# Where weight pieces begin, modulo 512 bytes, in a two-layer decoder trunk

## The chip, the core and the metric

The kernel runs on one core of a Trainium2 chip. The metric is the device time of one execution in microseconds (us). The kernel before was timed three times on one chip; the median is 609.84 us (609.62 to 609.87).

## The reference

Two identical layers and one final RMSNorm, on 256 tokens of 1024 channels in float32. Each layer reads one normalised input through one wide projection, runs three attention branches on it, and merges them with gates. Cut to what matters:

```python
def hybrid_layer(x, gain, w_in, f_bias, w_branch, w_out):
    h = rms_norm(x, gain)
    proj = jnp.einsum('bsd,de->bse', h, w_in)              # [256,1024] x [1024,9808]
    (qa, ka, va, ga, qb, kb_, vb_, gb, qc, kc, vc, gc,
     q_idx, k_idx, w_idx, f_logit, merge_logit) = jnp.split(proj, SPLIT_POINTS, axis=-1)
    oa = moba_attention(rope(qa), rope(ka), va) * silu(ga)
    ob = dsa_attention(rope(qb), rope(kb_), vb_, rope(q_idx), rope(k_idx), w_idx) * silu(gb)
    oc = forgetting_attention(qc, kc, vc, log_sigmoid(f_logit + f_bias)) * silu(gc)
    y = jnp.einsum('nbsw,nwd->bsnd', jnp.stack([oa, ob, oc]), w_branch)   # 3 x [512,1024]
    merged = jnp.sum(sigmoid(merge_logit).reshape(B, S, 3, D) * y, axis=2)
    return x + jnp.einsum('bsd,de->bse', merged, w_out)    # [1024,1024]
```

Each branch has 8 heads of 64 channels.

## The kernel before, in words

**Numbers in two pieces.** Every operand of a large matmul is split in a "hi" piece (rounded to TensorE's float32r) and a "lo" piece (what is left). A product is three matmuls: hi times hi, lo of the activations times hi of the weights, and hi of the activations times lo of the weights. The activations lie in `hTh` and `hTl` (normalised input), `og0h` to `og1l` (gated branch outputs) and, for the output projection, in the space of `V` (`v0`, `v1`). A weight piece is made from a loaded chunk `raw`: ScalarE writes the hi piece into a buffer `wh` (line 415), VectorE writes the lo piece into a buffer `wl` (line 419). There are six buffers of each, used in turn.

**Which operand stands still.** In `PE.matmul(out, a, b)` the array first loads `a`, 128 columns (the stationary operand; the profile shows this load as a row of its own, LDWEIGHTS on PEld), and then streams `b` past it (the moving operand). A row of the profile names the moving operand first: `proj<-hTh,wh` streams `hTh` past a weight piece, `proj<-wh,v` streams a weight piece past activations.

The kinds of units, by the letters that the change uses:

- B (`unit_b` on `win_b`; queries, keys, gates, indexer and merge logits): a weight piece is stationary, 256 columns of `hTh` or `hTl` move. Per layer 1,536 matmuls. `UNIT_ORDER` mixes hi and lo: six matmuls on hi pieces, one on lo, three on hi, one on lo, and so on.
- Y (`unit_y` on `wbr`; the branch projections): a weight piece is stationary, 256 columns of `og` move. Per layer 288.
- V (values of two branches) and O (output projection; O0 its left half of columns, O1 its right half), both `unit_a` on `rows_a`: activations are stationary, 512 columns of a weight piece move. At the very end, in the right half of the last layer, the second half of the tokens is done in two times 256 columns.
- C and CK (`va_units`; values of the third branch, 256 columns, and its other half with the small projections, 336 columns): activations are stationary, a weight piece moves (line 1132).

Between these stand the matmuls of attention: scores (lines 678 and 680), transposes of the probabilities in threes (line 766), and probabilities times values (lines 782 to 785).

**Where things begin.** The pool lays the buffers one behind the other in each partition. `wh0` begins at byte 1152, which is 128 modulo 512, and each buffer has 1152 words = 4608 = 9 x 512 bytes, so all `wh` begin at 128 and all `wl`, which come 384 bytes later than a multiple of that, at 0. By the same sum `V` and the queries begin at 128, and `hTh`, `hTl`, `og`, the block-diagonal keys `bd` and the transposed probabilities at 192 modulo 512. A buffer has 128 words more than a piece of 1024 words needs, so a piece can be moved inside it. `shifted` does that for moving pieces by the table `MOVING`; stationary pieces take the default, the buffer's start: hi at 128, lo at 0.

**What sets the order.** A planner (`Plan.run`) places every operation on an engine by costs, keys and a table `SHIFT`. It knows no addresses, so places inside a buffer do not enter it.

Of the kernel before, what the change touches and what calls it, by code (L numbers as in the profile page):

```python
# [32 lines left out]

R_RING = 6
R_RAW = 4
MOVING = {"V": (192, 192), "C": (128, 0), "CK": (384, 384), "O": (128, 128)}
TAIL = {"ACT": 95.0, "DVE": 85.0, "POOL": 0.0, "PE": 0.0, "SP": 0.0}
STEP = 24.0
SPLIT_LEAD = 2.0
# [237 lines left out]
def hybrid_trunk(ctx, tc, x, w_in, w_branch, w_out, final_gain, consts, out):  # L277
    nc = tc.nc
    PE, ACT, DVE, POOL = nc.tensor, nc.scalar, nc.vector, nc.gpsimd
# [13 lines left out]
    def T(b):  # L293
        return b.slot[1]
# [28 lines left out]
    V = [pool.tile([128, 2, 8, 128], F32R, name=f"v{i}") for i in range(2)]  # L323
# [67 lines left out]

    chunks, pieces = {}, {}

    def shifted(kind):
        at = MOVING[kind]
        return [slice((a - base) % 512 // 4, (a - base) % 512 // 4 + 1024) for a, base in zip(at, (128, 0))]

    def piece(key, ckey, ap, cshape, sel, shape, k, at=(slice(0, 1024), slice(0, 1024))):
        if key in pieces:
            return pieces[key]  # L400
        if ckey not in chunks:
            c = chunks[ckey] = Buf("raw")
            ca, cb = cshape

            def load():
                c.v = T(c)[:, :ca * cb].rearrange("p (a b) -> p a b", a=ca)
                nc.sync.dma_start(c.v, ap)
            dma(load, 512 * ca * cb * (1 if cb >= 128 else 2), [], [c], k - 12, f"dma {ckey}")
        c = chunks[ckey]
        a, b = shape  # L410
        p = pieces[key] = (Buf("wh"), Buf("wl"))

        def hi():
            p[0].v = T(p[0])[:, at[0]][:, :a * b].rearrange("p (a b) -> p a b", a=a)
            ACT.activation(p[0].v, sel(c.v), AF.Copy)  # L415

        def lo():
            p[1].v = T(p[1])[:, at[1]][:, :a * b].rearrange("p (a b) -> p a b", a=a)
            DVE.tensor_tensor(p[1].v, sel(c.v), p[0].v.bitcast(F32), op=ALU.subtract)  # L419
        act(hi, a * b, False, [c], [p[0]], k - SPLIT_LEAD, f"hi {key}")  # L420
        dve(lo, a * b, [c, p[0]], [p[1]], k - SPLIT_LEAD, f"lo {key}", port=True)
        return p
# [6 lines left out]
    def rows_a(kind, w, l, c0, i, k):  # L429
        src = w[l][(i // 2) * 512:(i // 2 + 1) * 512, c0:c0 + 512].rearrange("(k p) c -> p k c", p=128)  # L430
        a = (i % 2) * 2
        return piece((kind, l, c0, i), (kind, l, c0, i // 2), src, [4, 512], lambda r: r[:, a:a + 2, :], [2, 512], k,
                     shifted("O" if kind == "O" else "V"))

    def wbr(l, n, j, k):
        src = w_branch[l][n][:, (j // 2) * 256:(j // 2 + 1) * 256].rearrange("(k p) c -> p k c", p=128)
# [26 lines left out]
    def unit(name):  # L463
        units[0] += 1
        return units[0] - 1
# [560 lines left out]
    hA = (lambda k, t: hTh[:, k, t * 128:(t + 1) * 128], lambda k, t: hTl[:, k, t * 128:(t + 1) * 128])  # L1026
# [16 lines left out]

    def first_v():

        us, at = [unit("va0"), unit("va1")], shifted("V")
        ps = [Buf("proj"), Buf("proj")]
        left, done = [24, 24], [[], []]
        raws = [Buf("raw"), Buf("raw")]
        for i in range(KC):  # L1050
            c = raws[i // 4]
            if i % 2 == 0:
                ph, pl = Buf("wh"), Buf("wl")
            v = lambda b, w, i=i: T(b)[:, at[w]][:, (i % 2) * 512:(i % 2 + 1) * 512]
            rv = lambda c=c, i=i: T(c)[:, (i % 4) * 512:(i % 4 + 1) * 512]
            src = w_in[0][i * 128:(i + 1) * 128, COL["va"]:COL["va"] + 512]
            kr, kh, kl = Tok(), Tok(), Tok()
            plan.op([("SP", 512 * 512 / 330.0, lambda rv=rv, src=src: nc.sync.dma_start(rv(), src))], [], [kr], -95 + 0.2 * i, LAND,
                    f"dma va{i}", touch=[c])
            key = W_KEY[0] + W_KEY[1] * i  # L1060
            if i:
                key = max(key, HT_KEY[0] + HT_KEY[1] * (i - 0.5))
            plan.op([("ACT", t_act(512, False), lambda v=v, rv=rv, ph=ph: ACT.activation(v(ph, 0), rv(), AF.Copy)),
                     ("DVE", t_dve2(512), lambda v=v, rv=rv, ph=ph: DVE.tensor_copy(v(ph, 0), rv()))],
                    [kr], [kh], key, 0.0, f"hi va{i}", touch=[c, ph])
            dve(lambda v=v, rv=rv, ph=ph, pl=pl: DVE.tensor_tensor(v(pl, 1), rv(), v(ph, 0).bitcast(F32), op=ALU.subtract),
                512, [kr, kh], [kl], key + 0.05, f"lo va{i}", touch=[c, ph, pl], port=True)
            for t in range(2):
                for w, h, kw, kx, n in ((ph, hA[0], kh, 0, 0), (ph, hA[1], kh, 1, 0), (pl, hA[0], kl, 0, 1)):
                    def emit(t=t, w=w, h=h, i=i, v=v, n=n):  # L1070
                        left[t] -= 1
                        PE.matmul(T(ps[t]), h(i, t), v(w, n), start=left[t] == 23, stop=left[t] == 0)  # L1072
                    k = Tok()
                    done[t].append(k)
                    pe(emit, t_mm(512), [kw, k_hT[kx][t][i]], [k], us[t] - 10, f"va{t}", touch=[ps[t], w])
        for t in range(2):
            v_out(ps[t], t, 0, done[t], us[t])

    def va_units(l, vi):

        fine = False
        us, ats = [unit(f"vc{h}{t}") for h in "lr" for t in range(2)], [shifted("C"), shifted("CK")]

        def rows(raw, c, n, k0, k1, key):
            tok = Tok()
# [4 lines left out]
            return tok  # L1090

        def split(p, n, w, c, x0, x1, raw, cols, k0, reads, toks, key):
            dst = lambda i: T(p[i])[:, ats[w > 256][i]][:, :n * w].rearrange("p (k c) -> p k c", k=n)[:, x0:x1, c:c + cols]
            src = lambda: T(raw)[:, :8 * cols].rearrange("p (k c) -> p k c", k=8)[:, k0 + x0:k0 + x1]
            m = (x1 - x0) * cols
            ways = [("ACT", t_act(m, False), lambda: ACT.activation(dst(0), src(), AF.Copy))]
            if fine:
                ways.append(("DVE", t_dve2(m), lambda: DVE.tensor_copy(dst(0), src())))
            plan.op(ways, reads + [k_hT[1][0][KC - 1]], toks[0], key, 0.0, "hi va", touch=[raw, p[0]])
            dve(lambda: DVE.tensor_tensor(dst(1), src(), dst(0).bitcast(F32), op=ALU.subtract), m, reads + toks[0], toks[1],  # L1100
                key + 0.5, "lo va", touch=[raw, *p], port=True)

        for side, (w, slots) in enumerate(((256, ((0, 4), (4, 8))), (336, ((0, 3), (3, 6), (6, 8))))):
            u = us[2 * side:2 * side + 2]
            ps = [Buf("proj"), Buf("proj")]
            left, done = [24, 24], [[], []]
# [9 lines left out]
            for i, (a, b) in enumerate(slots):  # L1116
                p, n = [Buf("wh"), Buf("wl")], b - a
                tk = [[Tok() for _ in range(n)] for _ in range(2)]
                hk = VA_HI[2 * side + i] if fine else u[0] - SPLIT_LEAD
                for x0, x1 in ((0, 2), (2, 4)) if fine and not side and not i else ((0, n),):  # L1120
                    split(p, n, w, 0, x0, x1, raw, 256, a, list({id(kr[a + x]): kr[a + x] for x in range(x0, x1)}.values()),
                          [tk[0][x0:x1], tk[1][x0:x1]], hk)
                kt2 = [[Tok()], [Tok()]]
                if side:
                    split(p, n, w, 256, 0, n, rk, 80, a, [kk], kt2, hk)
                for t in range(2):
                    for wi, hi in ((0, 0), (0, 1), (1, 0)):
                        for js in [(x,) for x in range(n)] if fine and not side and not i else (range(n),):
                            def emit(t=t, wi=wi, hi=hi, js=js, p=p, n=n, a=a, w=w, ps=ps, left=left):
                                for x in js:  # L1130
                                    left[t] -= 1
                                    PE.matmul(T(ps[t])[:, :w], hA[hi](a + x, t), T(p[wi])[:, ats[w > 256][wi]][:, :n * w].rearrange(  # L1132
                                        "p (k c) -> p k c", k=n)[:, x], start=left[t] == 23, stop=left[t] == 0)
                            k = Tok()
                            done[t].append(k)
                            pe(emit, len(js) * (t_mm(w) + 4.6), [tk[wi][x] for x in js] + (kt2[wi] if side else []) +
                               [k_hT[hi][t][a + x] for x in js], [k], u[t] - (10 if fine else 0), f"v{side}{t}", touch=[ps[t], p[wi]])
# [44 lines left out]
    for l in range(L):  # L1182
# [31 lines left out]
        for hh in range(2):  # L1214
            gets = [lambda k, i=i: rows_a("O", w_out, l, hh * 512, i, k) for i in range(4)]
            for t in range(2):
                ra = [lambda k, p=p: [k_mg[k][p]] for p in range(2)]
                cols = [(0, 256), (256, 256)] if last and hh + t == 2 else [(0, 512)]
                for i, (c, n) in enumerate(cols):
                    u, ps = unit_a(f"o{hh}{t}", gets, t, mA[0], mA[1], ra, c, n)  # L1220
# [38 lines left out]
```

## Time and profile before

| what | value |
|---|---|
| median of 3 runs | 609.84 us |
| the profiled execution's own time | 609.88 us |
| its span, first to last instruction | 607.9 us |
| mean granted TensorE clock | 0.998 |
| TensorE matmuls | 4848 records, busy 599.9 us |
| VectorE, ScalarE, GpSimd busy | 534.3, 439.9, 89.7 us |
| DMA moved | 107.39 MB, 177 GB/s in the mean |

The end of a matmul is modelled in this profile: a row's duration runs past the start of the next matmul, and reads about 163 ns more than the step from one start to the next. So rates are read here from starts: the step from one matmul's start to the next one's. In the timeline a row with "x4" is four like matmuls in one line, and the step is the next row's start less its own, over four.

### The profile page before, as it was taken

Reading aid. Unit: us, or ns where it says so; the run is one execution under the profiler, and the core shown is the slowest. Engines: PE = TensorE matmul, PEld = TensorE weight load, DVE = VectorE, ACT = ScalarE, POOL = GpSimd, SP = SyncE. Lnnn points to the kernel's source line nnn. Section 1 sums busy time; section 2 is a strip of 40 time slices with the busy share of each in tenths; the row PEclk is TensorE's granted clock in tenths of the full one; section 3 lists DMA queues with packets and bytes.
Section 4 is the critical chain, followed back from the end, with each engine's and each line's share of the span. In section 5 each row is a group of like instructions: output and inputs, shape, how many; then the busy total and the mean of one; then the engine's idle time right before and its main releaser. Section 6 shows DMA issues by size and latency. Waiting matters only on the chain.

```text
span 607.9 us, 12752 instructions
## 1 busy us (share of the span) xinstructions
PE 599.9 (99%) x4848; PEld 581.7 (96%) x4848; DVE 534.3 (88%) x1340; ACT 439.9 (72%) x933; POOL 89.7 (15%) x97
## 2 busy tenths in 40 slices
PE   8999999999999999999999999999999999999996
PEld 6999999999998999999889999999999999999985
DVE  8899999997998899979586999999889978999873
ACT  6668669697986678775585875987788756986641
POOL 1032052000000334100000520320000014220000
PEclk9999999999999999999999999999999999999999
DMA  9995384845454655284547547557448256445411
GB/s 305 296 312 183 90 240 140 252 134 188 140 174 139 208 173 173 88 274 163 160 141 255 159 139 234 166 183 228 128 118 278 92 175 204 144 139 183 165 35 70
DMA packets 98109, 107.39 MB, mean 177 GB/s; under 512 B 4352, under 2 KB 88960, under 8 KB 98048
## 3 DMA queue, kind: packets, MB, share of 16 engines
q1 hardware_dynamic: 97760, 106.15, 55.4%
q8 instruction: 38, 0.62, 0.4%
q10 hardware_dynamic: 288, 0.43, 0.2%
q14 instruction: 23, 0.19, 0.1%
HBM read 103.42 MB, written 1.05 MB: 172 GB/s over the span
## 4 chain that ended last, share of the span: by engine, by line
PE 97%; issue 1%; DMA 1%; DVE 0%; ACT 0%; POOL 0%; POOLq 0%; DVEq 0%; SPq 0%
PE proj L457 80%; PE proj L1132 4%; PE t L766 3%; PE s L680 2%; PE s L678 2%; PE proj L1072 2%; PE o L785 1%; PE o L782 1%; DMA xg<-in_x_dram 1%; PE o L784 0%; PE o L783 0%; PE t L580 0%; PE s L580 0%; POOL fsum L626 0%; ACT tmp L565 0%
## 5 line engine op out<-in xcount | busy, mean ns | idle before, releaser
L457 PE MATMUL proj<-hTh,wh 128*128 128x256 f32 x1024 | 266.6, 278 | 0.0
L457 PE MATMUL proj<-hTl,wh 128*128 128x256 f32 x1024 | 265.8, 277 | 0.0
L419 DVE TENSOR_TENSOR wl<-raw,wh 128x1024 fp32r<-128x1024 f32 x180 | 221.9, 1240 | 29.1 <-ACT wh L415 26.5
L457 PE MATMUL proj<-hTh,wl 128*128 128x256 f32 x1024 | 230.6, 278 | 0.0
L415 ACT ACTIVATE wh<-raw 128x1024 fp32r<-128x1024 f32 x180 | 190.0, 1058 | 54.9 <-PE proj L457 50.2
L457 PEld LDWEIGHTS proj<-hTh,wh 128*128 128x128 f32 x1024 | 192.4, 188 | 0.1
L457 PEld LDWEIGHTS proj<-hTl,wh 128*128 128x128 f32 x1024 | 192.3, 188 | 0.1
L457 PEld LDWEIGHTS proj<-hTh,wl 128*128 128x128 f32 x1024 | 173.5, 188 | 0.0
L507 POOL TENSOR_TENSOR rsh<-rsh,cst 128x256 f32<-128x256 f32 x40 | 32.9, 823 | 323.4 <-DVE rsh L506 271.5
L509 POOL TENSOR_TENSOR rr<-rr,rsh 128x256 f32<-128x256 f32 x40 | 48.0, 1199 | 5.1 <-DVE rr L508 2.0
L743 ACT ACTIVATE e<-e,st 128x128 f32<-128x128 f32 (+1 forms) x96 | 42.7, 447 | 6.6 <-DVE st L739 6.3
L457 PE MATMUL proj<-wh,v 128*128 128x512 f32 (+1 forms) x144 | 35.2, 366 | 0.0
L457 PE MATMUL proj<-og0l,wh 128*128 128x256 f32 x128 | 33.8, 276 | 0.0
L457 PE MATMUL proj<-og0h,wh 128*128 128x256 f32 x128 | 32.3, 276 | 0.0
L457 PEld LDWEIGHTS proj<-wh,v 128*128 128x128 f32 x144 | 25.3, 189 | 4.2
L457 PE MATMUL proj<-og0h,wl 128*128 128x256 f32 x128 | 28.6, 276 | 0.0
L771 DVE TENSOR_TENSOR ptl<-t,pth 128x384 fp32r<-128x384 f32 x48 | 24.8, 550 | 0.7 <-ACT pth L769 0.5
L457 PEld LDWEIGHTS proj<-og0h,wh 128*128 128x128 f32 x128 | 24.0, 188 | 0.0
L457 PEld LDWEIGHTS proj<-og0l,wh 128*128 128x128 f32 x128 | 24.0, 188 | 0.0
L800 DVE TENSOR_TENSOR ot<-o,ot 64x256 f32<-64x256 f32 x48 | 19.9, 415 | 3.8 <-ACT ot L798 3.4
L769 ACT ACTIVATE pth<-t 128x384 fp32r<-128x384 f32 x48 | 21.8, 482 | 0.4
L457 PEld LDWEIGHTS proj<-og0h,wl 128*128 128x128 f32 x128 | 21.7, 188 | 0.0
(225 smaller groups left out, 1098.5 us busy)
## 6 DMA issues: line engine op xcount, KB each, us to landing
raw<-in_w_in_dram SPq DMA_DIRECT2D x74, 1024.0 KB, 5.3
raw<-in_w_branch_dram SPq DMA_DIRECT2D x24, 512.0 KB, 3.6
raw<-in_w_out_dram SPq DMA_DIRECT2D x8, 1024.0 KB, 5.1
raw<-in_w_in_dram SPq DMA_DIRECT2D x8, 256.0 KB, 5.4
tmp<-wf SPq DMA_DIRECT2D x16, 128.0 KB, 6.5
raw<-in_w_in_dram SPq DMA_DIRECT2D x2, 320.0 KB, 7.6
x<-in_x_dram SPq DMA_DIRECT2D x2, 256.0 KB, 4.9
acc<-in_final_gain_dram SPq DMA_DIRECT2D x1, 512.0 KB, 3.6
```

The lines of the kernel that those rows point to most:

```text
L415: ACT.activation(p[0].v, sel(c.v), AF.Copy)
L419: DVE.tensor_tensor(p[1].v, sel(c.v), p[0].v.bitcast(F32), op=ALU.subtract)
L457: PE.matmul(o(), a(), b(), start=first and i == 0, stop=last and i == n - 1)
L507: gps(lambda: POOL.tensor_tensor(T(sh)[:np_], T(sh)[:np_], s[:np_], op=ALU.mult), S, [k_rope], [sh], key, "rope")
L509: gps(lambda: POOL.tensor_tensor(T(r)[:np_], T(r)[:np_], T(sh)[:np_], op=ALU.add), S, [sh], [r], key, "rope")
L678: PE.matmul(o.rearrange("p (h c) -> p h c", h=2), qh[:, sl], kl[:, :, :n], start=True, stop=False)
L743: act(lambda t=t, a=a, n=n, e=e, st=st: ACT.activation(T(e)[:, a:a + n], T(e)[:, a:a + n], AF.Exp, bias=T(st)[:, t:t + 1], scale=-1.0, acc ...
L766: PE.transpose(T(ps)[:, i * 128:(i + 1) * 128], T(es[h])[:, i * 128:(i + 1) * 128], ident)
L769: act(lambda h=h, src=src: ACT.activation(T(ph)[:, h], src(), AF.Copy), 384, True, [ps], [kp[h][0]], key, "pT", touch=[ph])
L771: dve(lambda h=h, src=src: DVE.tensor_tensor(T(pl)[:, h], src(), T(ph)[:, h].bitcast(F32), op=ALU.subtract), 384, [ps, kp[h][0]], [kp[h][1 ...
L800: dve(lambda r=r, h=h: DVE.tensor_tensor(T(t)[r], T(o)[:64, h * S:(h + 1) * S], T(t)[r], op=ALU.add), S, [o], [kt[h]], key, "og", touch=[t ...
L1132: PE.matmul(T(ps[t])[:, :w], hA[hi](a + x, t), T(p[wi])[:, ats[w > 256][wi]][:, :n * w].rearrange("p (k c) -> p k c", k=n)[:, x], start=le ...
```

## The change

The table `MOVING` becomes `PLACE`, with an entry for every kind of unit and, in each, one pair (hi, lo) for layer 0 and one for layer 1. `piece` looks its own place up by kind and layer; `place` stands for `shifted`, and O is told apart by its half.

What begins elsewhere, in bytes modulo 512 (hi, lo):

| kind | before, both layers | layer 0 now | layer 1 now |
|---|---|---|---|
| B and Y (stationary) | 128, 0 | 128, 128 | 0, 0 |
| C (moving, 256 columns) | 128, 0 | 0, 0 | 128, 128 |
| O1 (moving) | 128, 128 | 128, 128 | 192, 192 |
| V, CK, O0 (moving) | 192, 192; 384, 384; 128, 128 | the same | the same |

Of the 4,832 matmuls 1,944 have an operand that begins elsewhere. Every engine has the same instructions in the same order with the same waits; no size, no count and no buffer changes. The transfers and what they load are the same too, since `raw` is untouched.

```diff
-MOVING = {"V": (192, 192), "C": (128, 0), "CK": (384, 384), "O": (128, 128)}
+PLACE = {"V": ((192, 192), (192, 192)),
+         "C": ((0, 0), (128, 128)),
+         "CK": ((384, 384), (384, 384)),
+         "O0": ((128, 128), (128, 128)),
+         "O1": ((128, 128), (192, 192)),
+         "B": ((128, 128), (0, 0)),
+         "Y": ((128, 128), (0, 0))}
...
-    def shifted(kind):
-        at = MOVING[kind]
-        return [slice((a - base) % 512 // 4, (a - base) % 512 // 4 + 1024) for a, base in zip(at, (128, 0))]
-
-    def piece(key, ckey, ap, cshape, sel, shape, k, at=(slice(0, 1024), slice(0, 1024))):
+    def place(kind, l):
+        at = PLACE[kind][l]
+        return [slice((a - base) % 512 // 4, 1152) for a, base in zip(at, (128, 0))]
+
+    def piece(key, ckey, ap, cshape, sel, shape, k):
+        at = place(key[0] if key[0] in PLACE else "V", key[1])
...
-        return piece((kind, l, c0, i), (kind, l, c0, i // 2), src, [4, 512], lambda r: r[:, a:a + 2, :], [2, 512], k,
-                     shifted("O" if kind == "O" else "V"))
+        return piece((f"{kind}{c0 // 512}" if kind == "O" else kind, l, c0, i), (kind, l, c0, i // 2), src, [4, 512], lambda r: r[:, a:a + 2, :], [2, 512], k)
...
+        def rows_of(p, i, n, w):
+            at = place("C" if w == 256 else "CK", l)[i]
+            return T(p[i])[:, at][:, :n * w].rearrange("p (k c) -> p k c", k=n)
...
-            dst = lambda i: T(p[i])[:, ats[w > 256][i]][:, :n * w].rearrange("p (k c) -> p k c", k=n)[:, x0:x1, c:c + cols]
+            dst = lambda i: rows_of(p, i, n, w)[:, x0:x1, c:c + cols]
```

More of the change, by code (lines that the diff above doesn't have):

```diff
@@ L1044, in first_v @@
     def first_v():
-        us, at = [unit("va0"), unit("va1")], shifted("V")
+        us, at = [unit("va0"), unit("va1")], place("V", 0)
         ps = [Buf("proj"), Buf("proj")]
@@ L1081, in va_units @@
         fine = False
-        us, ats = [unit(f"vc{h}{t}") for h in "lr" for t in range(2)], [shifted("C"), shifted("CK")]
+        us = [unit(f"vc{h}{t}") for h in "lr" for t in range(2)]
+        def rows_of(p, i, n, w):
+            at = place("C" if w == 256 else "CK", l)[i]
+            return T(p[i])[:, at][:, :n * w].rearrange("p (k c) -> p k c", k=n)
         def rows(raw, c, n, k0, k1, key):
@@ L1131, in emit @@
                                     left[t] -= 1
-                                    PE.matmul(T(ps[t])[:, :w], hA[hi](a + x, t), T(p[wi])[:, ats[w > 256][wi]][:, :n * w].rearrange(
-                                        "p (k c) -> p k c", k=n)[:, x], start=left[t] == 23, stop=left[t] == 0)
+                                    PE.matmul(T(ps[t])[:, :w], hA[hi](a + x, t), rows_of(p, wi, n, w)[:, x], start=left[t] == 23, stop=left[t] == 0)
                             k = Tok()
```

## The prediction

> **What bounds the kernel now.** I read the page first, then the chain of waits, then matmul starts in the timeline.
>
> ```profile
> span 607.9 us, 12752 instructions
> PE 599.9 (99%) x4848; PEld 581.7 (96%) x4848; DVE 534.3 (88%) x1340; ACT 439.9 (72%) x933; POOL 89.7 (15%) x97
> PEclk9999999999999999999999999999999999999999
> PE 97%; issue 1%; DMA 1%; DVE 0%; ACT 0%; POOL 0%; POOLq 0%; DVEq 0%; SPq 0%
> ```
>
> TensorE is the chain from end to end, at full clock, and stands waiting for nobody after the start. So the time is the number of matmuls times the step from one to the next, and a place that alters this step alters the time by just that. Nearly all matmuls that the change touches are these, in the view by groups of one shape (name, shape, count, busy us, mean ns):
>
> ```profile
> L457 PE MATMUL proj<-hTh,wh 128*128 128x256 f32 x1024 | 266.6, 278 | 0.0
> L457 PE MATMUL proj<-hTl,wh 128*128 128x256 f32 x1024 | 265.8, 277 | 0.0
> L457 PE MATMUL proj<-hTh,wl 128*128 128x256 f32 x1024 | 230.6, 278 | 0.0
> L457 PE MATMUL proj<-og0l,wh 128*128 128x256 f32 x128 | 33.8, 276 | 0.0
> L766 PE MATMUL t<-cst,e 128*128 128x128 f32 x144 | 21.6, 272 | 0.0
> L785 PE MATMUL o<-ptl,v 128*64 128x256 f32 x48 | 13.5, 281 | 0.0
> ```
>
> They go at one of two steps. The short step is in this long piece of the chain (start, length, count):
>
> ```profile
> 104.45 15.65 PE proj L457 x138
> ```
>
> 15.65 / 138 = 113.4 ns; hi at 128 and lo at 0 alternate, and the moving operand is at 192. The long step is seen behind the transposes of an attention head (timeline; start, duration):
>
> ```profile
> 160.06 0.36 PE L457 MATMUL proj<-hTh,wh 128*128 128x256 f32 x1
> 160.26 0.28 PE L457 MATMUL proj<-hTl,wh 128*128 128x256 f32 x1
> 160.38 0.28 PE L457 MATMUL proj<-hTh,wh 128*128 128x256 f32 x1
> 160.49 0.28 PE L457 MATMUL proj<-hTl,wh 128*128 128x256 f32 x1
> 160.61 0.28 PE L457 MATMUL proj<-hTh,wh 128*128 128x256 f32 x1
> 160.73 0.28 PE L457 MATMUL proj<-hTl,wh 128*128 128x256 f32 x1
> 160.85 0.28 PE L457 MATMUL proj<-hTh,wl 128*128 128x256 f32 x1
> ...
> 161.32 0.28 PE L457 MATMUL proj<-hTh,wl 128*128 128x256 f32 x1
> 161.43 0.28 PE L457 MATMUL proj<-hTl,wh 128*128 128x256 f32 x1
> ```
>
> From 160.26 to 160.85 are five steps in 0.59 us, 117.5 to 118 ns each, and they do not get faster. From 161.32 on, after lo pieces, it is 0.11 again. Behind a score the long step ends with the first lo pieces:
>
> ```profile
> 50.61 0.45 PE L678 MATMUL s<-bd0l,qh 128*128 128x512 f32 x1
> 50.90 0.28 PE L680 MATMUL s<-bd0h,qx 128*128 128x256 f32 x1
> ...
> 51.14 0.28 PE L457 MATMUL proj<-hTh,wh 128*128 128x256 f32 x1
> 51.26 0.28 PE L457 MATMUL proj<-hTl,wh 128*128 128x256 f32 x1
> 51.38 0.39 PE L457 MATMUL proj<-hTh,wl 128*128 128x256 f32 x2
> 51.60 0.28 PE L457 MATMUL proj<-hTh,wh 128*128 128x256 f32 x1
> ```
>
> 51.14 to 51.38 is 0.12 a step; the two on `wl` take 0.22 together. So I read the trace as two rhythms, both of which can hold: a stationary load and the moving stream beside it either fit or hinder each other. The load of the next weights runs beside the stream:
>
> ```profile
> 116.88 0.28 PE L457 MATMUL proj<-hTl,wh 128*128 128x256 f32 x1
> 116.99 0.28 PE L457 MATMUL proj<-hTh,wh 128*128 128x256 f32 x1
> 116.99 0.19 PEld L457 LDWEIGHTS proj<-hTl,wh 128*128 128x128 f32 x1
> ```
>
> An event (a score, a transpose, probabilities times values, a stretch of another shape) throws TensorE into the hindered rhythm. **In every stretch that I looked through, stationary pieces at 128 alone never led out of it once it had settled; pieces at 0 did, mostly within one or two.**
>
> That the relation of the two places matters is also in rows of other units of 256 columns, which never reach the short step:
>
> ```profile
> 21.24 0.63 PE L1132 MATMUL proj<-wh,hTh 128*128 128x256 f32 x4
> 21.71 0.64 PE L1132 MATMUL proj<-wh,hTl 128*128 128x256 f32 x4
> 22.18 0.64 PE L1132 MATMUL proj<-wl,hTh 128*128 128x256 f32 x4
> 22.65 0.63 PE L1132 MATMUL proj<-wh,hTh 128*128 128x256 f32 x4
> 597.02 0.64 PE L457 MATMUL proj<-wh,v 128*128 128x256 f32 x4
> 597.50 0.40 PE L457 MATMUL proj<-wl,v 128*128 128x256 f32 x2
> ...
> 601.34 0.64 PE L457 MATMUL proj<-wh,v 128*128 128x256 f32 x4
> ```
>
> C (moving at 128 or 0, stationary at 192): 0.47 / 4 = 117.5 ns. The end of O1 (both at 128): 0.48 / 4 = 120 ns, and still so 36 matmuls later (601.34 - 597.02 = 4.32 us).
>
> **The change part by part.**
>
> *Work of ScalarE and VectorE.* They write the same pieces elsewhere; nothing is added. Were they a little slower, TensorE's cover is that it does not wait for them now; I cost it at nothing.
>
> *B and Y in layer 0: lo goes from 0 to 128.* Every stationary piece then stands at 128, and the way out of the hindered rhythm is gone. A layer has 3,072 / 2 = 1,536 B and 288 Y matmuls, 1,824 in all. A long step costs 117.5 - 113.3 = 4.2 ns. How many are there? A layer has 16 scores (12 pairs of heads, 4 indexer units), 12 products with values (48 / 4) and 24 triples of transposes (144 / 6); some 43 stretches of B or Y lie between them. Stretches behind a score, a product with values, C/CK or V (1,164 of layer 0's 1,824 matmuls) all begin in the hindered rhythm. Of those behind transposes (the other 660) some four in ten go straight to the short step when they begin on pieces at 128 (both counts are from the starts in the timeline). So 1,164 + 0.6 x 660 = 1,560 long steps, 6.5 us. What is long already must be taken off: the mean duration of B is 277.7 ns against 276 of the `og` row, 1.7 x 3,072 = 5.2 us, of which about 40 steps of 0.20 instead of 0.11 behind transposes (160.06 to 160.26) are some 3.2 us and stay; 2.0 to 2.2 us for both layers are left, 1.1 us each. Net **+5.4 us**. Bounds: all 1,824 long is +6.5; if half of the stretches fall out at a boundary between units, +2.2; if the rhythm dies out by itself as now, 0; if one place for both pieces avoids it at all, -1.1.
>
> *B and Y in layer 1: hi goes from 128 to 0.* All stationary pieces are then such as led out of the hindered rhythm. Of today's 1.1 us I take away half: **-0.6 us**. Bounds: -1.1 if the long step vanishes; +6.5 if pieces at 0 alone can hold it, for which this speaks:
>
> ```profile
> 227.13 0.28 PE L457 MATMUL proj<-hTh,wh 128*128 128x256 f32 x1
> 227.25 0.40 PE L457 MATMUL proj<-hTh,wl 128*128 128x256 f32 x2
> 227.49 0.28 PE L457 MATMUL proj<-hTl,wh 128*128 128x256 f32 x1
> 227.60 0.28 PE L457 MATMUL proj<-hTh,wl 128*128 128x256 f32 x1
> ```
>
> The two on `wl` at 227.25 take 0.24, so a pair at 0 can have long steps too.
>
> *O1 in layer 1 goes from 128 to 192, its stationary `V` at 128.* This is the pairing of B. The last 48 matmuls of 256 columns take 120 ns; at 113.3 they save 0.32 us, at B's long 117.5 only 0.12. The 24 of 512 columns run at twice 113.3 and should stay. Against that stands the score at 50.61, the same pairing and 512 columns: 50.61 to 50.90, 287 ns, 60 more. But it follows two short matmuls, and its own load began just before it, so I put the 60 down to that load; if not, it is +1.4 us. I take **-0.2 us**.
>
> *C.* Pieces at 128 and at 0 both step at 117.5 (21.24 to 22.65): **0**, within 0.1.
>
> Sum: 5.4 - 0.6 - 0.2 = +4.6 us. The profiled execution took 609.88 us itself (span 607.9 and 2.0 around it), 0.04 above the median; so 609.88 + 4.6 = **614.5 us**.
>
> The Trainium skill speaks against all of this: "SBUF — State Buffer", section "Who interferes with whom", gives the matmul's moving operand and LDWEIGHTS a read port each, independent, and says that PE never waits on anyone. By that rule no place could matter and the time would stay 609.9. This trace does not agree: one shape steps at 113.4, 117.5 and 120 ns.
>
> **The rivals.**
>
> *The hindered rhythm does not outlast its few steps* (not slower). Place: B and Y of layer 0. Perhaps what ends it today is the step count or the turn from one unit to the next, not pieces at 0; the longest run on pieces at 128 that the trace can show is six matmuls, since `UNIT_ORDER` then puts a lo piece. Then layer 0 gains or loses some 0.5, layer 1 gains about 0.6, O1 0.2: 608.5 to 609.6, say **608.8 us**. It decides if more than about nine in ten of the hindered stretches end by themselves. Against it: C and the end of O1 hold their long step, C from 21.24 to 22.65, O1 for 36 matmuls and across two units.
>
> *Places differ in the first steps only by what stands before them, and nothing the change moves matters* (the change does not do what it is about). The sum of all terms is then within 0.3: **609.9 us**. Against it: 117.5 and 120 for one shape.
>
> *Pieces at 0 alone hold the hindered rhythm as well.* Layer 1 then pays like layer 0, up to +6.5 instead of -0.6: about **620 us**. For it: 227.25. Against it: most pairs on `wl` lead out, as at 51.38.
>
> **How the numbers follow.** The forecast (layer 0 stuck, layer 1 not) 0.62; no sticking 0.19; no effect 0.12; both layers stuck 0.07. The forecast's own range is 611.3 (609.88 + 2.2 - 0.8) to 616.4 (609.88 + 6.5, with no gain in layer 1 and O1). The range on record goes down to 608.3 to take in the two rivals below it, and leaves the last one out. A difference of 0.2% (1.2 us) is about what a measurement of this kernel can tell from no change. Slower by more: 0.62 + 0.07 = 0.69, less a little for small cases, 0.67. The second rival's 608.5 to 609.6 is mostly within 0.2% and in part below; with a gain of more than 1.2 us at 0.15, the rest, 0.18, is no change.
>
> **What would show it.** In the chain of waits the piece of 138 at 104.45 takes 138 x 117.5 ns = 16.2 instead of 15.65 us if it is stuck, and long pieces of layer 1 stay at 113.4 ns a matmul. The mean duration of B's rows reads 280 in layer 0's windows and 276 to 277 in layer 1's. The last units step below 120 ns. ScalarE's and VectorE's splits keep their durations. The forecast is wrong if layer 0's long pieces still run at 113.4 ns; it is wrong upward if layer 1's run at 117.5.

## The result, and the profile after

The changed kernel takes **617.17 us** (median of 4 runs, 617.07 to 617.62), the kernel before on the same chip 609.81 us (609.62 to 609.87). The ratio is 1.0123, with a 95% interval of 1.0111 to 1.0136. The change costs 7.4 us, 2.8 us more than the 4.6 that were forecast.

The lines of the page after that answer to those of before: span, busy time by engine, TensorE's granted clock, and the shares of the chain of waits.

```profile
span 615.1 us, 12752 instructions
PE 607.0 (99%) x4848; PEld 589.5 (96%) x4848; DVE 536.0 (87%) x1340; ACT 440.0 (72%) x933; POOL 89.2 (14%) x97
PEclk9999999999999999999999999999999999999999
PE 96%; issue 1%; ACT 1%; DMA 1%; DVE 0%; POOL 0%; POOLq 0%; DVEq 0%; SPq 0%
L463 PE MATMUL proj<-hTh,wh 128*128 128x256 f32 x1024 | 269.2, 280 | 0.0
L426 DVE TENSOR_TENSOR wl<-raw,wh 128x1024 fp32r<-128x1024 f32 x180 | 221.8, 1239 | 30.7 <-ACT wh L422 27.9
L422 ACT ACTIVATE wh<-raw 128x1024 fp32r<-128x1024 f32 x180 | 189.9, 1057 | 58.9 <-PE proj L463 52.3
```

The span is 7.2 us longer, and TensorE's busy time 7.1. The clock is the same, and matmuls still make up the chain. ScalarE's and VectorE's splits take 1057 and 1239 ns; before they took 1058 and 1240:

```profile
L419 DVE TENSOR_TENSOR wl<-raw,wh 128x1024 fp32r<-128x1024 f32 x180 | 221.9, 1240 | 29.1 <-ACT wh L415 26.5
L415 ACT ACTIVATE wh<-raw 128x1024 fp32r<-128x1024 f32 x180 | 190.0, 1058 | 54.9 <-PE proj L457 50.2
```

So the whole loss is in the step from one matmul to the next. Long pieces of the chain show where (start, length, count; the middle of the program, where layer 0 ends, is near 309). First after:

```profile
72.83 17.67 PE proj L463 x150
101.22 4.09 PE proj L463 x36
106.01 16.25 PE proj L463 x138
...
408.86 14.29 PE proj L463 x126
...
493.22 32.19 PE proj L463 x240
```

The same pieces before, apart from the one shown with the prediction:

```profile
72.04 17.04 PE proj L457 x150
402.41 14.32 PE proj L457 x126
486.81 31.32 PE proj L457 x240
```

In layer 0 the piece of 138 takes 16.25 us, 117.75 ns a matmul, from its first to its last, where it took 113.4. The 36 at 101.22 are one of three stretches of layer 0 that run at the short step (4.09 / 36 = 113.6 ns). In layer 1 the piece of 126 is at the short step as before, but the piece of 240 has grown by 0.87 us. It is 36 matmuls of V followed by 204 of B.

The timeline of after shows the two sides of layer 1. Behind a product with values the hindered rhythm ends after three steps; behind V it does not end:

```profile
408.70 0.28 PE L463 MATMUL proj<-hTh,wh 128*128 128x256 f32 x1
408.82 0.28 PE L463 MATMUL proj<-hTl,wh 128*128 128x256 f32 x1
...
409.05 0.28 PE L463 MATMUL proj<-hTl,wh 128*128 128x256 f32 x1
...
409.73 0.28 PE L463 MATMUL proj<-hTh,wh 128*128 128x256 f32 x1
...
501.22 0.28 PE L463 MATMUL proj<-hTh,wh 128*128 128x256 f32 x1
501.34 0.28 PE L463 MATMUL proj<-hTl,wh 128*128 128x256 f32 x1
...
501.93 0.28 PE L463 MATMUL proj<-hTh,wl 128*128 128x256 f32 x1
...
502.52 0.28 PE L463 MATMUL proj<-hTl,wh 128*128 128x256 f32 x1
```

From 408.70 to 409.05 are three steps, 117 ns in the mean, and from 409.05 to 409.73 six of 113 ns. Behind V, from 501.22 to 502.52, are eleven in 1.30 us, 118 ns each, and so it goes on for all 204. Every stationary piece there begins at 0.

Because a matmul's end is modelled, sizes are taken from starts. For each layer I add up, over its 1,824 B and Y matmuls, the step to the next start less 113.33 ns, and call the sum the layer's **excess**. Left out are the steps of 0.20 us, the first ones behind transposes, which the change leaves as they were (22 in layer 0 with 1.9 us, before and after). The "free share" is the share of steps of 113 or 114 ns.

| kernel | excess layer 0 (free) | excess layer 1 (free) | last 48 matmuls of 256 columns in O1 | C, each layer |
|---|---|---|---|---|
| before | 1.13 us (0.85) | 1.09 us (0.86) | 0.31 us | 0.22 us |
| after | 7.44 us (0.07) | 2.28 us (0.72) | 0.21 us | 0.21 to 0.22 us |

O1's 24 matmuls of 512 columns in layer 1 take 0.07 us longer than before, so O1 gains 0.03 in all. The sum is 6.31 + 1.19 - 0.03 = 7.5 us, and 7.4 were measured.

### The profile page after: what moved, and what is told of

Read it like the earlier page. It is cut to its first block, busy times and chain, and to the rows that moved or that the text cites. A ratio compares the mean times of both kernels' runs of the same rounds, so it can differ in the third digit from the quotient of the medians.

```text
span 615.1 us, 12752 instructions
## 1 busy us (share of the span) xinstructions
PE 607.0 (99%) x4848; PEld 589.5 (96%) x4848; DVE 536.0 (87%) x1340; ACT 440.0 (72%) x933; POOL 89.2 (14%) x97
## 4 chain that ended last, share of the span: by engine, by line
PE 96%; issue 1%; ACT 1%; DMA 1%; DVE 0%; POOL 0%; POOLq 0%; DVEq 0%; SPq 0%
PE proj L463 80%; PE proj L1142 4%; PE t L772 3%; PE s L686 2%; PE s L684 2%; PE proj L1078 2%; PE o L791 1%; PE o L788 1%; DMA xg<-in_x_dram 1%; PE o L790 0%; PE o L789 0%; ACT hTh L593 0%; PE t L586 0%; PE s L586 0%; ACT acc L536 0%
## 5 line engine op out<-in xcount | busy, mean ns | idle before, releaser
L426 DVE TENSOR_TENSOR wl<-raw,wh 128x1024 fp32r<-128x1024 f32 x180 | 221.8, 1239 | 30.7 <-ACT wh L422 27.9
L463 PE MATMUL proj<-hTh,wl 128*128 128x256 f32 x1024 | 233.1, 280 | 0.0
L422 ACT ACTIVATE wh<-raw 128x1024 fp32r<-128x1024 f32 x180 | 189.9, 1057 | 58.9 <-PE proj L463 52.3
L804 ACT ACTIVATE ot<-o 64x256 f32<-64x256 f32 x48 | 18.3, 381 | 5.3 <-PE o L791 4.6
```

The costliest lines, as they stand in the source:

```text
L463: PE.matmul(o(), a(), b(), start=first and i == 0, stop=last and i == n - 1)
L804: act(lambda r=r, h=h: ACT.activation(T(t)[r], T(o)[64:, h * S:(h + 1) * S], AF.Copy), S, True, [o], [kt[h]], key, "og", touch=[t], half=True)
```

## The experiments

All start from the new code with the table set back to the places of before, and change entries of it. Y always gets B's places, and the diffs show B's line only. Every kernel computes the whole reference. The theory under test is **holding**: an event throws TensorE into the hindered rhythm, some turns of places lead out of it, and a stretch that does not get out pays 4.2 to 4.4 ns a matmul to its end. Its rivals are a **price per matmul** (every matmul whose neighbours have the same place pays, whatever its history), and the prediction's third rival, that pieces at 0 alone hold the rhythm too.

### Which part of the change costs what

Layer 0 alone:

```diff
-         "B": ((128, 0), (128, 0)),
+         "B": ((128, 128), (128, 0)),
```

> Only layer 0's B and Y get hi and lo at 128; all else as before. Holding theory (a hindered rhythm that only a turn of places ends, so each layer pays for its own stretches): layer 0's B and Y go from 1.1 to 7.4 us above the short step, layer 1 stays at 1.1, in all 609.8 + 6.3 = 616.1 us. Rival (the two layers, O1 and C act together, or what is lost comes by ScalarE and VectorE writing elsewhere): another sum than 6.3 for this part, say 2 to 5 us.

Layer 1 alone:

```diff
-         "B": ((128, 0), (128, 0)),
+         "B": ((128, 0), (0, 0)),
```

> Only layer 1's B and Y get hi and lo at 0. Holding theory: layer 1's B and Y go from 1.1 to 2.3 us above the short step, layer 0 stays, in all 611.0 us; the long steps lie behind V, behind C/CK and behind some transposes, not behind scores and products with values. Rival (layer 1 is only late from what layer 0 did): no change, 609.8.

C and O1 alone, as in the change:

```diff
-         "C": ((128, 0), (128, 0)),
+         "C": ((0, 0), (128, 128)),
...
-         "O1": ((128, 128), (128, 128)),
+         "O1": ((128, 128), (192, 192)),
```

> Only C and O1 are moved as in the change; B and Y as before. Holding theory: nothing to tell, 609.8 less 0.0 to 0.2 us (the end of O1 from 306 to some 210 ns above the short step, 0.07 more in its 512-column part, C the same). Rival (part of the loss is theirs): up to 611.

Measured, beside the kernel before at 609.90 us on the same chip:

| run | time us | ratio, 95% interval | excess l0, l1 us |
|---|---|---|---|
| layer 0 | 616.18 | 1.0106 (1.0090 to 1.0121) | 7.44, 1.08 |
| layer 1 | 611.23 | 1.0020 (1.0011 to 1.0030) | 1.14, 2.28 |
| C and O1 | 609.93 | 1.0003 (0.9994 to 1.0011) | 1.13, 1.08 |

The parts add up: 6.28 + 1.33 + 0.03 = 7.64 us against 7.36. Each excess is the one that the layer had in the whole change, so the layers do not act on each other. The chain of waits of the run with layer 0 alone:

```profile
73.08 17.67 PE proj L463 x150
106.26 16.25 PE proj L463 x138
```

and of the run with layer 1 alone:

```profile
104.68 15.65 PE proj L463 x138
487.44 32.19 PE proj L463 x240
```

The first has layer 0's long pieces at the long step, the second has them at the short one and its V stretch with the 0.87 us more. **Layer 1's part costs 1.3 us; the forecast had it gain 0.6.** C is worth nothing, and O1's end gains 0.1 us of which its wider part gives back most.

### Held state or price per matmul

In layer 0 every second unit of B has its lo piece at 128 (256 of the 512 lo matmuls), the others at 0 as before:

```diff
         at = place(key[0] if key[0] in PLACE else "V", key[1])
+        if key[0] == "B" and key[1] == 0 and key[3] == 0:
+            at = [slice(0, 1152), slice(32, 1152)]
```

> As before, but in layer 0 every second B unit (24 matmuls) has lo at 128 like hi; Y and layer 1 as before. Holding theory: a unit without a turn keeps whichever rhythm it finds, the next unit with lo at 0 turns it out; some 20 of 43 stretches meet such a unit hindered and keep it for some 12 to 18 more matmuls of 4.2 ns: +1.0 us, 610.8 (0.5 to 1.8 more). Rival (each matmul whose weights stand at the place of those before it pays): half of the changed kernel's cost in B, +2.7 us, 612.5. Rival (a turn of places within some units is enough for all): no change, 609.8.

Measured: 610.88 us, ratio 1.0015 (1.0006 to 1.0025), beside 609.76. Layer 0's excess is 2.23 us, its free share 0.71. In the chain of waits, the pieces with 17.67 and 16.25 us above:

```profile
72.36 17.01 PE proj L465 x150
104.80 15.73 PE proj L465 x138
```

Half of B's lo pieces at 128 cost 1.1 us, as the holding theory expected (1.0), and not the 2.7 of a price per matmul. Stretches that cross a unit with a lo piece at 0 run at the short step again, right through the later units that have none: the piece of 138 begins with some 20 long steps and then goes at the short one, 15.73 / 138 = 114 ns in the mean. A price per matmul is out, and what costs is a state that ends, in most cases, when a turn of places comes along. The interval, from 1.0006, also rules out the second rival, that a turn within some units is enough for all.

### Where layer 1's loss sits

Pieces of layer 1 at 0 as in the change, but the first unit of B behind C/CK and the first behind V turn between 0 and 128:

```diff
+        if key[0] == "B" and key[1] == 1 and key[3] == 0 and key[2] in (COL["qi"], COL["qb"]):
+            at = [slice(96, 1152), slice(32, 1152)]
```

> As the run with layer 1's B and Y all at 0, but the first B unit after C/CK and the first after V in layer 1 have lo at 128. Holding theory: what layer 1 lost is held stretches, above all the 204 matmuls after V and the 42 after CK; a turn in their first unit frees them: layer 1's B and Y from 2.28 to some 1.3 us above the short step, 611.2 - 1.0 = 610.2 us. Rival (pieces at 0 cost a little everywhere): two of some 76 units change, no difference to tell, 611.2.

Measured: 609.81 us, ratio 1.0002 (0.9992 to 1.0011), beside 609.74. Layer 1's excess falls from 2.28 to 1.25 us. The chain of waits of this kernel, the V stretch and the piece of 126:

```profile
402.50 14.29 PE proj L465 x126
486.86 31.32 PE proj L465 x240
```

The V stretch is back at 31.32 us, as before, and the units after the first stand at 0 alone and stay at the short step. So pieces at 0 can hold either rhythm, the long one included, and behind V and behind C/CK one unit that turns is enough to leave it. The stretches behind transposes that had no such unit (60, 42 and 18 matmuls) stay long in this kernel.

### Is it which piece, or that they differ

hi at 0 and lo at 128, in both layers:

```diff
-         "B": ((128, 0), (128, 0)),
+         "B": ((0, 128), (0, 128)),
```

> B and Y of both layers have hi at 0 and lo at 128, the pair of before turned round. Holding theory: places alternate as before, so the rhythm is turned out as before, 609.8 with 0.7 either way. Rival (128 itself is a bad place and 0 a better one for any stationary piece, whatever stands next to it): two thirds of the pieces are at 0 now, one third was; by the changed kernel's 7.4 and 2.3 us a layer the third at 128 would cost 4.0 us a layer, 615.6.

Measured: 609.47 us, ratio 0.9991 (0.9982 to 1.0000), excess 1.08 and 0.94 us. Which piece stands where makes a difference of 0.15 us a layer at most; that they take turns is what counts for B and Y.

### Other places

One place for both pieces, another one in each layer. Each of these kernels was timed once, beside 609.74 to 609.76 us before. The edits, in the order of the expectations:

```diff
+         "B": ((64, 64), (256, 256)),
+         "B": ((192, 192), (320, 320)),
+         "B": ((384, 384), (448, 448)),
+         "B": ((160, 160), (96, 96)),
+         "B": ((32, 32), (224, 224)),
```

> B and Y with hi and lo at 64 in layer 0 and at 256 in layer 1 (moving operands stay at 192). If only the distance moving less stationary modulo 512 sets the step: 256 has C's hi distance (448), which in the profile before never reached the short step, so layer 1 should have all 1,824 near 117.5 ns, 7.6 us above the short step. 64 has distance 128, which no row shows: between 1 and 12 us. Rival (the operands' kind matters, not the distance: what is stationary weights behaves alike at each place): both layers between 1 and 7.4, free stretches in both.

> B and Y with hi and lo at 192 in layer 0 and at 320 in layer 1. By distance: 192 is the end of O1's (0), 120 ns each without a free stretch, 1,824 x 6.7 = 12.2 us above the short step in layer 0. 320 (distance 384) is shown by no row: between 1 and 12 us. Rival (kind of operand, not distance): layer 0 between 1 and 7.4.

> B and Y with hi and lo at 384 in layer 0 and at 448 in layer 1. By distance: 384 is that of C's lo pieces (320), some 118 ns, 8.5 us above the short step in layer 0. 448 (distance 256) is shown by no row: between 1 and 12 us. Rival (kind of operand, not distance): layer 0 between 1 and 7.4.

> B and Y with hi and lo at 160 in layer 0 and at 96 in layer 1, between the places run so far, which repeated after 256 bytes (0 as 256: 2.3 us above the short step; 64 as 320: 10; 128 as 384: 7.4; 192 as 448: 11.8). If places count in steps of 64: 160 as 128 or as 192 (7.4 or 11.8), 96 as 64 or as 128 (10 or 7.4). Rival (the distance counts byte by byte, with a best place in between): under 2 us, or between the neighbours.

> B and Y with hi and lo at 32 in layer 0 and at 224 in layer 1. In steps of 64: 32 as 0 or as 64 (2.3 or 10), 224 as 192 or as 256 (11.8 or 2.3). Rival (byte by byte): under 2 us, or between the neighbours.

Measured: 620.24, 629.56, 626.59, 625.73 and 625.33 us. Ordered by the distance from the stationary piece to the moving one (192 less the place), taken modulo 256:

| distance mod 256 | places (layer) | excess us | free share |
|---|---|---|---|
| 0 | 192 (0), 448 (1) | 11.80, 11.80 | 0.00 |
| 32 | 160 (0) | 6.41 | 0.09 |
| 64 | 128 (0), 384 (0) | 7.44, 7.44 | 0.07 |
| 96 | 96 (1) | 11.78 | 0.01 |
| 128 | 64 (0), 320 (1) | 10.10, 10.00 | 0.01 |
| 160 | 32 (0) | 8.98 | 0.00 |
| 192 | 0 (1), 256 (1) | 2.28, 2.28 | 0.72, 0.68 |
| 224 | 224 (1) | 8.91 | 0.01 |

The two long pieces, of 138 in layer 0 and of 126 in layer 1, in the chain of waits with 64 and 256:

```profile
107.20 16.37 PE proj L463 x138
...
411.99 14.29 PE proj L463 x126
```

with 192 and 320:

```profile
107.62 16.56 PE proj L463 x138
...
415.80 14.95 PE proj L463 x126
```

and with 384 and 448:

```profile
106.04 16.25 PE proj L463 x138
...
411.75 15.12 PE proj L463 x126
```

16.56 / 138 and 15.12 / 126 are both 120.0 ns; 16.37 / 138 and 14.95 / 126 are both 118.6, a mean of single steps that go from 112 to 124 ns there; 384 gives 128's 16.25 to the hundredth, and 256 gives 0's 14.29.

So where the stationary piece begins counts **modulo 256 bytes**, not 512. In these runs the moving operand stays at 192. That it is the distance that counts, and not the place of the stationary piece alone, rests on the other kinds: O1's end with both at 128 has 120 ns, like B with both at 192; O1's end at 192 on 128 has 117.8, like B in layer 0; and C of layer 0 in the changed kernel, at 0 on 192, again a distance of 64, has 117.9 in the mean and not the 120 of B on 192. Other distances were not tried with another moving place.

By distance 192 came near what was expected (12.2 us, measured 11.8), 384 less so (8.5, measured 7.4) and 256 not at all. I had expected 256 to cost 7.6 us, since C's hi pieces (moving at 128, stationary at 192, which is 64 the other way like 192 to 256) have the long step throughout; it cost what 0 costs. C always follows V, behind which B's pieces at 0 keep the long step too; that this is why C never leaves it, no run shows. At the same place as the moving operand (distance 0) nearly every step is 119 to 121 ns, as the end of O1 showed before. The four places that are no multiple of 64 fit no simple picture: 96 is above both its neighbours, 160 below both. The mean step at 96 is 120 ns too, so the same place is not the only slowest one. How fine the grain is stays open.

### A better version?

Turns in both layers as in the swapped run, and O1 in layer 1 with hi at 192, lo at 320, so that it turns as well:

```diff
-         "O1": ((128, 128), (128, 128)),
-         "B": ((128, 0), (128, 0)),
+         "O1": ((128, 128), (192, 320)),
+         "B": ((0, 128), (0, 128)),
```

> B and Y with hi at 0 and lo at 128 in both layers (the swapped pair, 0.1 us a layer less than before), and O1 of layer 1 with hi at 192 and lo at 320, so that the last units' places alternate like B's. Holding theory: the end of O1 goes from 306 to under 100 ns above the short step; 609.9 - 0.2 - 0.2 = 609.4 us, 0.1% below before. Rival (the two halves of O1 hinder each other in the 512-column part as at the swap of halves): no gain, 609.7.

Measured: 609.66 us, ratio 0.9999 (0.9991 to 1.0008), excess 1.07 and 0.94, O1's end 0.20 us. The expectation for O1 failed. Its places take turns between the distances 64 and 192, as B's do, and it stays near the long step; its 24 matmuls of 512 columns take 0.10 us longer than before, so O1 gains nothing, as the rival said. C in the kernel before takes turns between the same two distances and keeps the long step too, through all 48 matmuls of a layer (0.22 us). So turns led out only where weight pieces are stationary. No version beat the kernel before by more than can be measured. Of its 2.2 us of excess the places tried here took away 0.2 at most.

## Why the prediction was right or wrong

**Direction and mechanism.** The reading that the hindered rhythm holds from event to event when no turn of places ends it was right: the piece of 138 takes 16.25 us, 16.2 was forecast; the run with every second unit rules out a price per matmul. With it the first two rivals fall, "does not outlast its few steps" by the 204, 138 and 150 matmuls that all keep the long step, and "nothing the change moves matters" by the runs with one layer alone. The excess of before, taken as 1.1 us a layer, measures 1.13 and 1.09.

**Layer 0, +5.4 forecast, +6.3 measured: a term mis-sized.** The count was 1,560 long steps, with four in ten of those matmuls that follow transposes going straight to the short step. Now 3 of 22 such stretches do (36, 78 and 24 matmuls, 138 of 660), and 1,686 steps are long. That is 126 x 4.2 = 0.5 us. The long step is 117.75 ns, 4.4 above the short one and not 4.2; 1,686 x 0.2 = 0.35 us. Together that is the 0.9 that was missed. The four in ten was high already in the trace of before, by the starts there: of the stretches behind transposes that begin with a hi piece, at 128, three of 11 in layer 0 go straight to the short step (at 39.86, 125.60 and 258.06), and five of 13 in layer 1. In the changed kernel it is again three of those 11, though others. None of the 11 that begin with a lo piece does, and these stand at 128 now too; the share was applied to their 294 matmuls as well. What decides which stretch goes free, no run shows. Those that do stay at the short step to their end, so pieces at 128 hold either rhythm.

**Layer 1, -0.6 forecast, +1.2 measured: the step with the wrong sign.** "Half of today's 1.1 us" was right in sign for what it spoke of: behind scores the rhythm now ends after two to four steps, behind products with values after two or three, and outside the stuck stretches the excess is 0.66 us, where it was 0.98 in the same stretches before. What failed is the sentence that pieces at 0 led out of the rhythm. They lead out of it behind scores, behind products with values and in most cases behind transposes. Behind V and behind C/CK they hold it: 204 matmuls with 0.91 us, 42 with 0.19, and behind transposes stretches of 60, 42 and 18 with 0.26, 0.18 and 0.08, in sum 1.62 us, where these five had 0.11 before. So the term is +1.51 - 0.32 = +1.2 us. The third rival was therefore right in its mechanism and wrong in its extent, for it had all of layer 1 stuck. I priced the term by two ends, -1.1 and +6.5, and gave the middle no chance of its own: pieces at 0 that hold only what some events leave behind. The row at 227.25 spoke for it. Which events leave it behind could not be seen in the trace of before, where pieces at 0 always turn with pieces at 128; the lengths of the stretches behind each kind of event could, and with them the price: 204 and 42 matmuls behind V and C/CK, at 4.2 ns, are 1.0 us.

**O1, -0.2 forecast, -0.03 measured.** The last matmuls step at 117.8 ns instead of 120, the smaller of the two savings that were worked out (0.12). The timeline of after shows it over 36 matmuls, 608.57 - 604.33 = 4.24 us against 4.32:

```profile
604.33 0.63 PE L463 MATMUL proj<-wh,v 128*128 128x256 f32 x4
604.80 0.40 PE L463 MATMUL proj<-wl,v 128*128 128x256 f32 x2
...
608.57 0.63 PE L463 MATMUL proj<-wh,v 128*128 128x256 f32 x4
```

It is B's pairing in layer 0, moving less stationary 64, and it has B's long step. The 512-column part lost 0.07 us, far from the +1.4 that the score would have given.

**C, 0 forecast, 0 measured. The splits, nothing forecast, nothing measured.** TensorE stayed the chain, so no cover was needed.

**The signs named for it.** The mean durations of B were to read 280 in layer 0's half and 276 to 277 in layer 1's. The groups of after in the first half of the span:

```profile
L463 PE MATMUL proj<-hTh,wh 128*128 128x256 f32 x512 | 135.2, 281 | 0.0
L463 PE MATMUL proj<-hTl,wh 128*128 128x256 f32 x512 | 135.1, 279 | 0.0
```

and in the second:

```profile
L463 PE MATMUL proj<-hTh,wh 128*128 128x256 f32 x512 | 133.9, 280 | 0.0
L463 PE MATMUL proj<-hTl,wh 128*128 128x256 f32 x512 | 133.3, 277 | 0.0
```

They do part, but by 1 to 2 ns where the steps of the two layers part by 2.8 ns in the mean ((7.44 - 2.28) us over 1,824). The durations hold a modelled end and were a poor sign; the chain's pieces and the starts were the good ones.

**The size of the whole.** Of the 2.8 us between 4.6 and 7.4, layer 1 is 1.8, layer 0 is 0.9 and O1 0.2 (0.1 more in sum, as the excesses come to 7.5). The forecast's own upper end took layer 0's bound (6.5) with no gain in layer 1. It left layer 1's bound to a rival with a chance of 0.07, and so the range stopped short of a partly stuck layer 1.

## What to carry to other kernels

Where TensorE is the chain, measure the step between matmul starts per stretch, not the mean duration, and look whether the step depends on where the operands begin. If it does, do not line all stationary pieces up at one place: turning between two places of which one leads out of the hindered rhythm kept 85% of the steps short here, and one such unit behind V and behind C/CK freed the units after it. This was so for B and Y alone: C and O1, whose weights are the moving operand, took turns between the same distances and stayed slow. A place that looks harmless within a mixed order must be priced alone, from every kind of event that it can follow.

## What the hardware showed that was not expected

One and the same matmul (128 x 128 against 256 columns) has a mean step of 113.3, 117.75, 118.6 or 120 ns by where its two operands begin and by what stood before it. The place of the stationary piece counts modulo 256 bytes: four pairs of places 256 apart gave the same excess within 0.1 us. From 609.5 to 629.6 us, the spread is 3.3% of the kernel with every instruction and wait unchanged. The Trainium skill's "SBUF — State Buffer", section "Who interferes with whom", has independent read ports for the two operands; the runs at 192 and 448, with 120 ns a step, do not agree. That the ports are where the two meet, no run shows.

At a distance of 192 both rhythms hold by themselves (and at 64, by layer 0's three free stretches), 113.4 ns for 126 matmuls behind a product with values and 118 ns for 204 behind V, in one run and with the same operands. Why the stretches behind V and C/CK stay hindered and those behind scores do not, and what in the load and the stream makes the two rhythms, no run here shows. That a load and a stream hinder each other remains inferred from the steps.
